# Placing identity, page pool and small vectors so that all matmul operands start at one residue of 512 bytes

## The chip, the cores and the metric

The kernel runs on one core of a Trainium2 chip. Five engines work side by side: TensorE (matmuls, transposes; the profile lists its weight loads apart, as PEld), VectorE (DVE), ScalarE (ACT), GpSimd (POOL) and SyncE (SP), which issues nearly all the DMAs here. Operands lie in the core's SBUF: 128 partitions, and in each a range of bytes; a tile has the same byte address in every partition. TensorE takes both operands from SBUF, the stationary one (loaded as weights, 128 columns) and the moving one (up to 512 columns), and writes to PSUM.

The metric is device microseconds of one execution, start to end. The kernel before takes 1100.9 us, the median of 3 runs (1098.44 to 1102.69 us).

## The reference

One encoder block over 1024 tokens of width 1024, in float32:

```python
n = rms_norm(h, norm1_g)
proj = n @ w_in                                   # 1024 x 2304: qa ka va qb kb vb
ya = mixer_a(qa, ka, va, sinks)                   # sliding window, ALiBi, sinks; 8 heads, 2 kv heads
yb = mixer_b(qb, kb, vb, rel_bias)                # own chunk + 8 before, relative bias; 8 heads
y = concatenate([rms_norm(ya, ga), rms_norm(yb, gb)])
h = h + y @ w_out                                 # 1024 x 1024
n2 = rms_norm(h, norm2_g)
u = square(relu(n2 @ w_ff1))                      # 1024 x 4096
h = h + u @ w_ff2                                 # 4096 x 1024
out = rms_norm(h, final_g)
```

## The kernel before

Every projection is a product of float32 accuracy made of three products of a shorter type: an operand is split into a high part (a copy of it, rounded) and a low part (what is left), and `mm3` (line 152) issues high x high, high x low and low x high, each a matmul with a stationary operand of 128 columns and a moving one of 512. `mm3` is called for the input projections (names `ip_...`), the output projection (`op_A`, `op_B`) and both MLP layers (`f`, and `f_a`, `f_b`, `f_c`). Scores (`S_...`) and the products of probabilities and V (`av_...`) are matmuls with 256 to 512 moving columns, and the probabilities are turned by transposes (`pt_...`; line 129), in which the data is the stationary operand and the identity the moving one, 128 columns.

The stages in time: input projections of the first heads (from 5 us on), attention with the other projections laid between its steps by a filler, output projection and second norm, the MLP's first layer (to about 778 us), its second layer with the final norm. Both MLP layers save an eighth of the products: seven products of half-size operands in place of eight, whose operands are sums of quarters. In the first layer (`product1`, line 907) the weights W are stationary and the transposed activations X are moving; in the second (`product2`, line 1072) the activations U are stationary and the weights V moving. A product of the second layer is 24 matmuls; the seven products are done for two slices of 512 each at a time, in the order of `order2` (line 1013). Operands are prepared two products ahead: VectorE makes the sums (T for the first layer, Z for the second, line 868), ScalarE copies the high parts (line 890), GpSimd or VectorE subtracts the low ones (line 132).

The order on every engine is set by the program's text, and on TensorE bound to it by `pe` (line 117). DMAs go through SP's one queue in order.

Tiles come from pools, and a pool's place in SBUF is set by the order in which pools are opened and by what each holds. In bytes per partition:

- `cp` (line 73), opened first: the identity (512 bytes), then the small vectors `ones`, `eps4`, `nsink`, `psink`, `ogc`, `g1c`, `warm` and `r1`, 32 bytes each.
- `main` (line 74): 35 pages of 4096 bytes (`page`, tag `pg`), 3 stage tiles (`stage`, tag `ws`) and 2 tiles of tag `tst`, 4096 bytes each. Pages hold the normed input nT, the projections' weights, Q, K, V, y, X, the high parts of W, u, w, C and more.
- `small` (line 75): statistics of one to eight columns, 32 bytes each at least, four buffers of a name; and a pad of 32 bytes (line 104).
- after `small`, one after another in the same place: `sp` (first loads), `at` (attention: the probabilities P, their turned parts T, bias, Y), `mp` (first layer: `page2`, tag `pg2`, with the low parts of W, and T and k), `fp` (second layer: `page3`, tag `pg3`).

In the second layer the first seven products have U and the high part of V in pages and the low part of V in a page or a stage tile; from the eighth on U (high and low) and the high part of V are of `page3`, the low part of V a stage tile (`high` and `third`, lines 1032 and 1033). Every slice that a matmul of the projections or the MLP takes out of a tile starts at a multiple of 512 bytes in it, so the residue of its address by 512 is that of its tile.

Of the kernel before, what the change touches and what calls it, by code (L numbers as in the profile page):

```python
# [8 lines left out]
F32 = mybir.dt.float32  # L9
# [6 lines left out]
P = 128  # L16
# [3 lines left out]
TB = SEQ // P  # L20
# [23 lines left out]
def kernel(  # L44
# [27 lines left out]

    cp = ctx.enter_context(tc.tile_pool(name="cp", bufs=1))
    main = ctx.enter_context(tc.tile_pool(name="main", bufs=1))
    small = ctx.enter_context(tc.tile_pool(name="small", bufs=4))
    dp = ctx.enter_context(tc.tile_pool(name="dp", bufs=1, space=DRAM))

# [3 lines left out]
    def page(shape, name, dt=F32R):  # L81
        return main.tile(shape, dt, tag="pg", bufs=NPAGES, name=name)
# [3 lines left out]

    ident = cp.tile([P, P], F32, name="ident")
    make_identity(nc, ident)
    ones = cp.tile([P, 1], F32, name="ones")
    nc.vector.memset(ones, 1.0)  # L90
    eps4 = cp.tile([P, 1], F32, name="eps4")
    nc.vector.memset(eps4, EPS / 4)
    nsink = cp.tile([P, 8], F32, name="nsink")
    psink = cp.tile([P, 8], F32, name="psink")
    ogc = cp.tile([P, 8], F32, name="ogc")
    g1c = cp.tile([P, 8], F32, name="g1c")
    nc.scalar.dma_start(g1c, norm1_g)
    warm = cp.tile([P, 1], F32, name="warm")
    nc.scalar.activation(warm, eps4, AF.Sqrt)

    last_load = [None]


    small.tile([P, 8], F32, tag="pad", bufs=1, name="pad")

    def load(dst, src, mark=False):

# [26 lines left out]
    def rstd(ss, n, width, name, r=None):  # L134

        if r is None:
            r = small.tile([P, width], F32, tag=f"rs{width}", name=f"r_{name}")
        u = small.tile([P, width], F32, tag=f"ru{width}", name=f"u_{name}")
        w = small.tile([P, width], F32, tag=f"rw{width}", name=f"w_{name}")
        q = small.tile([P, width], F32, tag=f"rq{width}", name=f"q_{name}")  # L140
        nc.scalar.activation(u, ss, AF.Sqrt, bias=eps4, scale=1.0 / (4 * n))
        nc.vector.tensor_scalar(w, ss, 1.0 / (4 * n), EPS / 4, ALU.mult, ALU.add)
        nc.vector.reciprocal(q, u)
        if width == 1:
            nc.vector.tensor_scalar(w, w, q, u, ALU.mult, ALU.add)
        else:
            nc.vector.tensor_tensor(w, w, q, ALU.mult)
            nc.vector.tensor_tensor(w, w, u, ALU.add)
        nc.vector.reciprocal(r, w)
        return r  # L150
# [37 lines left out]
    sp_ = ExitStack()  # L188
    sp = sp_.enter_context(tc.tile_pool(name="sp", bufs=1))
    sps = sp_.enter_context(tc.tile_pool(name="sps", bufs=1, space=PSUM))  # L190
    r1 = cp.tile([P, TB], F32, name="r1")
    R1 = page([P, SEQ], "R1", F32)
    xT_src = xT.rearrange("(k p) s -> p k s", p=P)
    nT = [[[page([P, 2, HALF], f"nT{t}{hl}{g}") for g in range(4)] for hl in range(2)] for t in range(2)]
# [13 lines left out]
    def token_scales(t):  # L208

        ss = small.tile([P, 4], F32, tag="ss4", name=f"ss1_{t}")  # L210
        for b in range(4):
            tb = 4 * t + b
            xr = sp.tile([P, D], F32, tag="xr", bufs=4, name=f"xr{tb}")
            load(xr, x[tb * P : (tb + 1) * P, :], True)
            nc.scalar.activation(xr, xr, AF.Square, accum_out=ss[:, b : b + 1])
        rstd(ss, D, 4, f"n1_{t}", r1[:, 4 * t : 4 * t + 4])
# [404 lines left out]
    def group_rstd(kind, psum, tag, bufs, r):  # L621
        ps = psum.tile([P, TB], F32, tag=tag, bufs=bufs, name=f"ss_{kind}")
        for tb in range(TB):
            matmul(ps[:, tb : tb + 1], sq[kind][:, tb * P : (tb + 1) * P], ones, start=True, stop=True)
        return rstd(ps, HALF, TB, f"g{kind}", r)
# [166 lines left out]
    def rows2(tb):  # L792

        h = hres.pop(tb)
        ps = flat(opb.pop(tb))
        nc.vector.scalar_tensor_tensor(ps, ps, rB[:, tb : tb + 1], h, ALU.mult, ALU.add)
        ss = small.tile([P, 1], F32, tag="ss", name=f"ss2_{tb}")
        nc.scalar.activation(h, ps, AF.Square, accum_out=ss)
        r = rstd(ss, D, 1, f"n2_{tb}")
        nc.scalar.activation(h, ps, AF.Copy)  # L800
        nc.sync.dma_start(hB[tb // 2][:, tb % 2], h)
        if tb in (4, 5):
            rows[tb] = main.tile([P, 2, HALF], F32, tag="tst", bufs=2, name=f"n2_{tb}")
        else:
            rows[tb] = page2([P, 2, HALF], f"n2_{tb}")
        nc.vector.scalar_tensor_tensor(flat(rows[tb]), ps, r, g2b, ALU.mult, ALU.mult)
# [394 lines left out]
def build(arrays):  # L1201
    import concourse.bacc as _bacc

    nc = _bacc.Bacc("TRN2", target_bir_lowering=False, num_devices=1)
    args = [nc.dram_tensor(f"in_{n}_dram", arrays[n].shape, F32, kind="ExternalInput").ap() for n in _INS]
    args.append(nc.dram_tensor("out_0_dram", (SEQ, D), F32, kind="ExternalOutput").ap())
    with tile.TileContext(nc, schedule_with_timeline_sim=True) as tc:
        kernel(tc, *args)
    return nc
# [9 lines left out]
```

## Time and profile before

| | before |
|---|---|
| median of 3 runs | 1100.9 us (1098.44 to 1102.69) |
| the profiled execution | 1100.78 us |
| its span, first to last instruction | 1099.0 us |
| TensorE busy | 1070.6 us, 97% |
| VectorE busy | 762.8 us, 69% |
| ScalarE busy | 530.4 us, 48% |
| GpSimd busy | 405.9 us, 37% |
| mean granted clock of TensorE | 0.997 of full |

A matmul's own duration in the profile is mostly latency, since matmuls are pipelined: one of 512 columns lasts 0.39 us and the next starts after 0.23 us. What a matmul costs in a row of them is therefore read from start to start: the start of a piece of the timeline less the start of the piece before, over the number of matmuls in it. In the chain of waits a piece's length is already counted so.

### The profile page before, as it was taken

The numbers are of one execution on the slowest core, as the hardware profiler recorded it, in microseconds if no ns is written. First come the engines' busy times: TensorE is split into PE (matmuls) and PEld (weight loads), VectorE is DVE, ScalarE is ACT, GpSimd is POOL, SyncE is SP. The second block draws the span as 40 slices with busy tenths as digits, with TensorE's granted clock in tenths as the row PEclk, the third lists the DMA queues.
The fourth block names the chain that finished last, engine by engine and source line by source line (L and its number), as shares of the span: only waits on it lengthen the run. The fifth ranks groups of instructions, "written<-read, shape, count | busy, mean of one in ns | idle before, by whom it ended". The sixth has DMA issues, their size and how long they took to land.

```text
span 1099.0 us, 14402 instructions
## 1 busy us (share of the span) xinstructions
PE 1070.6 (97%) x5088; PEld 879.8 (80%) x5088; DVE 762.8 (69%) x1170; ACT 530.4 (48%) x942; POOL 405.9 (37%) x248
## 2 busy tenths in 40 slices
PE   8998999999999999999999999999999999999997
PEld 6787878888878888778888888888787888888885
DVE  5577787767667766976755655646969777778667
ACT  7666765666564565553333333334333333333346
POOL 1365664343260231044553464445114024024025
PEclk9999999999999999999999999999999999999999
DMA  9943626353584342313354334516997535532004
GB/s 343 247 126 111 156 73 168 98 138 99 132 267 174 135 153 96 116 58 136 134 171 172 139 129 158 186 58 231 346 405 262 172 117 158 176 111 92 1 1 153
DMA packets 90584, 170.30 MB, mean 155 GB/s; under 512 B 7824, under 2 KB 43664, under 8 KB 90512
## 3 DMA queue, kind: packets, MB, share of 16 engines
q1 hardware_dynamic: 90368, 169.38, 46.7%
q8 instruction: 40, 0.66, 0.2%
q14 instruction: 32, 0.26, 0.1%
q10 hardware_dynamic: 144, 0.00, 0.0%
HBM read 105.39 MB, written 45.09 MB: 137 GB/s over the span
## 4 chain that ended last, share of the span: by engine, by line
PE 79%; DVE 10%; DMA 6%; issue 2%; ACT 2%; SPq 1%; DVEq 0%; ACTq 0%
PE f L126 25%; PE f_a L126 13%; PE f_c L126 6%; PE op_B L126 4%; PE ip_kB L126 4%; PE op_A L126 4%; PE f_b L126 3%; PE ip_qB L126 3%; PE ip_vB L126 3%; PE av_B L126 3%; PE ip_qA L126 2%; PE S_B L126 2%; PE pt_B L129 2%; DMA w<-in_w_ff_dram 2%; DVE Z L868 1%
## 5 line engine op out<-in xcount | busy, mean ns | idle before, releaser
L126 PE MATMUL f<-X,W 128*128 128x512 f32 x1344 | 316.1, 395 | 0.7 <-DVE k L936 0.7
L126 PEld LDWEIGHTS f<-X,W 128*128 128x128 f32 x1344 | 252.4, 189 | 56.1 <-issue 1.1
L126 PE MATMUL f_a<-V,U 128*128 128x512 f32 x768 | 180.5, 394 | 0.3 <-DVE V L132 0.3
L126 PEld LDWEIGHTS f_a<-V,U 128*128 128x128 f32 x768 | 144.1, 188 | 34.8 <-DVE V L132 0.7
L132 POOL TENSOR_TENSOR U<-u,U 128x1024 fp32r<-128x1024 f32 x32 | 81.0, 2531 | 234.9 <-PE f_c L126 140.9
L132 POOL TENSOR_TENSOR W<-T,W 128x1024 fp32r<-128x1024 f32 x32 | 82.9, 2591 | 163.2 <-ACT W L890 163.2
L126 PE MATMUL f_c<-V,U 128*128 128x512 f32 x384 | 90.3, 394 | 0.0
L126 PEld LDWEIGHTS f_c<-V,U 128*128 128x128 f32 x384 | 72.1, 188 | 16.9
L890 ACT ACTIVATE V<-Z 128x1024 fp32r<-128x1024 f32 x32 | 34.0, 1062 | 98.5 <-PE f_a L126 46.6
L132 POOL TENSOR_TENSOR W<-w,W 128x1024 fp32r<-128x1024 f32 x24 | 59.7, 2489 | 40.4 <-ACT W L890 37.6
L132 DVE TENSOR_TENSOR V<-w,V 128x1024 fp32r<-128x1024 f32 x24 | 47.9, 1998 | 28.4 <-ACT V L890 28.4
L890 ACT ACTIVATE V<-w 128x1024 fp32r<-128x1024 f32 x24 | 25.5, 1062 | 86.5 <-issue 36.3
L932 ACT ACTIVATE k<-f 128x1024 f32<-128x1024 f32 x24 | 24.7, 1028 | 81.6 <-PE f L126 81.6
L890 ACT ACTIVATE U<-u 128x1024 fp32r<-128x1024 f32 x56 | 58.5, 1044 | 8.7 <-DMA u<-ud 8.7
L388 ACT ACTIVATE P_B<-P_B,nm_B 128x640 f32<-128x640 f32 (+2 forms) x64 | 44.3, 693 | 25.6 <-DVE nm_B L387 13.2
L126 PE MATMUL ip_kB<-nT,w_kB 128*128 128x512 f32 x192 | 52.4, 402 | 3.1 <-DVE ts_qA L240 2.3
L890 ACT ACTIVATE W<-T 128x1024 fp32r<-128x1024 f32 x32 | 33.8, 1058 | 41.5 <-PE f L126 29.7
L126 PE MATMUL op_A<-w_o,y 128*128 128x512 f32 x192 | 52.1, 397 | 0.2 <-DVE h L705 0.2
L126 PE MATMUL ip_vB<-nT,w_vB 128*128 128x512 f32 x192 | 51.9, 398 | 0.0
L126 PE MATMUL ip_qB<-nT,w_qB 128*128 128x512 f32 x192 | 51.3, 395 | 0.0
L126 PE MATMUL ip_qA<-nT,w_qA 128*128 128x512 f32 x192 | 50.2, 399 | 0.9 <-DVE ts_qA L240 0.9
L132 DVE TENSOR_TENSOR V<-Z,V 128x1024 fp32r<-128x1024 f32 x32 | 46.2, 1447 | 6.8 <-ACT V L890 6.3
(208 smaller groups left out, 2018.9 us busy)
## 6 DMA issues: line engine op xcount, KB each, us to landing
w<-in_w_ff_dram SPq DMA_DIRECT2D x64, 512.0 KB, 4.5
u<-ud SPq DMA_DIRECT2D x56, 512.0 KB, 5.0
ud<-k SPq DMA_DIRECT2D x48, 512.0 KB, 2.7
KkB<-ts_kB SPq DMA_DIRECT2D x64, 128.0 KB, 2.3
yd<-y SPq DMA_DIRECT2D x14, 512.0 KB, 2.8
y<-yd SPq DMA_DIRECT2D x14, 512.0 KB, 7.1
xs<-in_xT_dram SPq DMA_DIRECT2D x16, 256.0 KB, 4.8
xr<-in_x_dram SPq DMA_DIRECT2D x8, 512.0 KB, 7.3
```

Of the source, the lines that this page charges most:

```text
L126: pe(nc.tensor.matmul(*args, **kw))
L129: pe(nc.tensor.transpose(*args))
L132: engine.tensor_tensor(lo, full, f(hi), ALU.subtract)
L388: nc.scalar.activation(pr[:, :n], pr[:, :n], AF.Exp, bias=nm, scale=-1.0, accum_out=sm)
L868: engine.tensor_tensor(t, a, b, op)
L890: nc.scalar.activation(w[0], full, AF.Copy)
L932: nc.scalar.activation(kept[p], ps, AF.Copy)
```

## The change

The identity stays in `cp` alone; the other small vectors go to a new pool `cv`, opened after `main`; the pad in `small` grows from 8 to 120 columns, and the scratch of `rstd` (u, w, q) gets two buffers in place of four. Nothing else is edited.

```diff
     cp = ctx.enter_context(tc.tile_pool(name="cp", bufs=1))
     main = ctx.enter_context(tc.tile_pool(name="main", bufs=1))
+    cv = ctx.enter_context(tc.tile_pool(name="cv", bufs=1))
     small = ctx.enter_context(tc.tile_pool(name="small", bufs=4))
...
     ident = cp.tile([P, P], F32, name="ident")
     make_identity(nc, ident)
-    ones = cp.tile([P, 1], F32, name="ones")
+    ones = cv.tile([P, 1], F32, name="ones")
...
-    g1c = cp.tile([P, 8], F32, name="g1c")
+    g1c = cv.tile([P, 8], F32, name="g1c")
...
-    small.tile([P, 8], F32, tag="pad", bufs=1, name="pad")
+    small.tile([P, 120], F32, tag="pad", bufs=1, name="pad")
...
-        u = small.tile([P, width], F32, tag=f"ru{width}", name=f"u_{name}")
-        w = small.tile([P, width], F32, tag=f"rw{width}", name=f"w_{name}")
-        q = small.tile([P, width], F32, tag=f"rq{width}", name=f"q_{name}")
+        u = small.tile([P, width], F32, tag=f"ru{width}", bufs=2, name=f"u_{name}")
+        w = small.tile([P, width], F32, tag=f"rw{width}", bufs=2, name=f"w_{name}")
+        q = small.tile([P, width], F32, tag=f"rq{width}", bufs=2, name=f"q_{name}")
...
-    r1 = cp.tile([P, TB], F32, name="r1")
+    r1 = cv.tile([P, TB], F32, name="r1")
```

The built program has the same instructions in the same order on every engine, with the same waits. What differs is the addresses (first byte of a partition, and that modulo 512):

| | before | after |
|---|---|---|
| identity | 16512, residue 128 | 16512, residue 128 |
| first page (35 pages, 4096 bytes each) | 17280, residue 384 | 17024, residue 128 |
| first stage tile (3, then 2 of `tst`) | 160640, residue 384 | 160384, residue 128 |
| start of `sp`, `at`, `mp`, `fp` | 184064, residue 256 | 183936, residue 128 |

The tiles in `sp`, `at`, `mp` and `fp` are 2048, 2560 or 4096 bytes, multiples of 512, so all of them share the residue of the pool's start.

## Rows read from the trace of the kernel before

**Rows 1.** The page: its span, and busy time of each engine.
```profile
span 1099.0 us, 14402 instructions
...
PE 1070.6 (97%) x5088; PEld 879.8 (80%) x5088; DVE 762.8 (69%) x1170; ACT 530.4 (48%) x942; POOL 405.9 (37%) x248
```

**Rows 2.** Chain of waits in the MLP: start us, length us, what, how many.
```profile
495.00 260.72 PE f L126 x1128
755.78 3.43 DVE T L868
...
798.54 10.15 DMA gfb<-in_final_norm_g_dram
808.76 11.46 DMA w<-in_w_ff_dram
...
844.94 22.43 PE f_a L126 x95
867.37 11.20 PE f_c L126 x48
...
1068.97 22.42 PE f_a L126 x96
```

**Rows 3.** Stretches: PE, PEld, DVE, ACT, POOL busy, clock, DMA share, GB/s.
```profile
495.00:755.80 260.80, 260.80 (x1131) 213.34 (x1130) 152.15 (x105) 91.36 (x91) 120.72 (x49) 1.00 0.43 152
755.80:845.00 89.20, 88.17 (x386) 71.94 (x384) 76.18 (x56) 32.58 (x33) 25.50 (x10) 1.00 0.84 310
845.00:1091.00 246.00, 246.00 (x1055) 197.99 (x1055) 182.56 (x165) 98.07 (x126) 68.82 (x32) 1.00 0.34 112
```

**Rows 4.** Waits of TensorE's MLP matmuls: total us, times, longest us.
```profile
PE f L126 <- DVE k L936: 0.7, 1, 0.7
...
PE f_a L126 <- DVE V L132: 0.3, 1, 0.3
```

**Rows 5.** TensorE's timeline, second layer's beginning: start us, us, matmuls.
```profile
778.70 11.04 PE L126 MATMUL f_a<-V,U 128*128 128x512 f32 x48
789.58 11.04 PE L126 MATMUL f_c<-V,U 128*128 128x512 f32 x48
...
822.28 11.15 PE L126 MATMUL f_a<-V,U 128*128 128x512 f32 x48
833.27 11.15 PE L126 MATMUL f_b<-V,U 128*128 128x512 f32 x48
...
844.94 5.39 PE L126 MATMUL f_a<-V,U 128*128 128x512 f32 x22 [0.30 <-DVE V L132]
```

**Rows 6.** Two stretches of the second layer, columns as in rows 3.
```profile
779.00:811.00 32.00, 32.00 (x143) 26.50 (x142) 28.18 (x23) 13.67 (x14) 6.86 (x2) 1.00 1.01 379
...
960.00:1065.00 105.00, 105.00 (x452) 84.51 (x451) 74.23 (x53) 37.71 (x38) 26.59 (x11) 1.00 0.17 56
```

**Rows 7.** Chain of waits, projections and transposes, to the first layer's start.
```profile
46.69 2.07 PE ip_qA L126 x9
...
122.75 1.37 PE ip_qB L126 x6
...
165.09 1.40 PE ip_kB L126 x6
...
438.65 0.44 PE tp L129 x4
...
444.57 10.93 PE op_B L126 x48
...
474.87 1.39 PE f L126 x6
```

**Rows 8.** TensorE's timeline, input projections.
```profile
30.22 5.60 PE L126 MATMUL ip_qA<-nT,w_qA 128*128 128x512 f32 x24
35.66 1.53 PE L126 MATMUL ip_vA<-nT,w_vA 128*128 128x512 f32 x6
```

**Rows 9.** The largest group of transposes: count, busy us, mean ns, idle before.
```profile
L129 PE MATMUL pt_B<-ident,P_B 128*128 128x128 f32 x240 | 42.2, 274 | 4.2 <-DMA y<-yd 2.4 <-DVE T_B L132 1.0 <-DVE rc_B L556 0.7
```

More of the change, by code (lines that the diff above doesn't have):

```diff
@@ L88 @@
     make_identity(nc, ident)
-    ones = cp.tile([P, 1], F32, name="ones")
+    ones = cv.tile([P, 1], F32, name="ones")
     nc.vector.memset(ones, 1.0)
-    eps4 = cp.tile([P, 1], F32, name="eps4")
+    eps4 = cv.tile([P, 1], F32, name="eps4")
     nc.vector.memset(eps4, EPS / 4)
-    nsink = cp.tile([P, 8], F32, name="nsink")
-    psink = cp.tile([P, 8], F32, name="psink")
-    ogc = cp.tile([P, 8], F32, name="ogc")
-    g1c = cp.tile([P, 8], F32, name="g1c")
+    nsink = cv.tile([P, 8], F32, name="nsink")
+    psink = cv.tile([P, 8], F32, name="psink")
+    ogc = cv.tile([P, 8], F32, name="ogc")
+    g1c = cv.tile([P, 8], F32, name="g1c")
     nc.scalar.dma_start(g1c, norm1_g)
-    warm = cp.tile([P, 1], F32, name="warm")
+    warm = cv.tile([P, 1], F32, name="warm")
     nc.scalar.activation(warm, eps4, AF.Sqrt)
+    small.tile([P, 120], F32, tag="pad", bufs=1, name="pad")
     last_load = [None]
-    small.tile([P, 8], F32, tag="pad", bufs=1, name="pad")
     def load(dst, src, mark=False):
```

## The prediction

> **What bounds the kernel now.** I read the busy shares first, to see which engine the span belongs to; then the chain of waits in order of time, to see where another engine holds TensorE up; then TensorE's timeline, for what one matmul costs in each stretch. The span is 1099.0 us of a profiled run of 1100.78 us, and TensorE is busy for 1070.6 us of it [rows 1]. From 495.00 to 755.78 us and from 844.94 us to the last matmul near 1091 us the chain is TensorE alone; between the two it runs over VectorE and DMA [rows 2]. VectorE has room in both TensorE stretches, 152.15 of 260.8 us and 182.56 of 246 us [rows 3]. The MLP's matmuls wait for an operand only twice, 0.7 and 0.3 us [rows 4]. So the time is the number of matmuls times what one costs, and this change touches neither the number nor the order: only the byte addresses of the operands.
>
> What the reader is to see is that a 128x512 matmul doesn't cost the same everywhere. In the second layer, 48 matmuls start at 778.70 us and the next 48 at 789.58 us: 10.88 / 48 = 226.7 ns each [rows 5]. From 822.28 to 833.27 us it is 10.99 / 48 = 229.0 ns [rows 5]. From 867.37 us to the end 48 take 11.20 us, 233.3 ns [rows 2]. In the first layer 1128 take 260.72 us, 231.1 ns [rows 2]. The granted clock is 1.00 in all these stretches (the 2.4 GHz level) [rows 3, 6], so the clock doesn't explain it. Nor does traffic: the fast stretch, 779 to 811 us, has the DMA engines full (1.01) and VectorE at 28.18 of 32 us, while 960 to 1065 us has DMA at 0.17 and is slow [rows 6].
>
> The placement does fit. Before the change a page lies at residue 384 of 512 bytes, a stage tile too, the attention and MLP pools at 256, the identity at 128. In the first layer X and the high weights are pages and the low weights lie at 256: 231.1 ns. In the second layer the first seven products have all operands in pages and stage tiles, and these are the matmuls of 226.7 ns; from the eighth on U and high V come from the pool at 256 and low V from a stage tile at 384: 229.0, later 233.3 ns. The output projection, whose weights and y are pages, takes 10.93 us for 48, 227.7 ns [rows 7]. The loads of the next weights overlap the running matmul (TensorE's two rows are 213.34 and 260.80 us in 260.8 us [rows 3]), so two reads of SBUF go on at once. I take it that where they start at different residues a matmul loses up to 6.7 ns more; that is a reading of three levels, and rival 1 is the other reading.
>
> **The change part by part.** The instruction lists, their order and their waits are those of before, engine by engine, so no operation is added, removed or moved. Three edits have one answer, nothing: the small vectors go to another pool, the pad grows, and the scratch of rstd gets two buffers in place of four (no wait appears in the built program, so no DVE or ACT row has cause to change). What is left is that identity, pages, stage tiles and the two big pools all come to residue 128.
>
> First layer: 1128 matmuls from 231.1 to 226.7 ns: 260.72 - 1128 x 0.22667 = 5.0 us. In the 22 us before it they stand in sixes behind transposes, such sixes at 1.39 us (the one at 474.87 us) against 6 x 226.7 = 1.36 [rows 7]; twelve of them, 0.3 us. This all lies on the chain.
>
> Second layer from 844.94 us: 95 + 864 + 96 = 1055 matmuls (the rows from 844.94, from 867.37 to 1068.97, and the last [rows 2]), at 233.3 to 226.7 ns: 1055 x 6.67 = 7.0 us. Cover for it: VectorE would be at 182.56 of 239 us.
>
> Between 755.78 and 844.94 us I count no gain. Its 386 matmuls would give up some 0.7 us (96 still of the first layer at 4.4 ns each, 168 of the second at none, 122 at 2.3), but the chain there is VectorE's T and Z, the load of gfb and the loads of w [rows 2], VectorE is busy 76.18 of 89.2 us and DMA 0.84 [rows 3], and TensorE arrives to find V missing at 844.94 us. It would only wait longer. The whole stretch is set off by a matmul at 755.78 us and so moves forward with the first layer; if its DMAs didn't, up to the 5 us would be lost there (second rival).
>
> Attention and projections, 0 to 473 us: about 1250 projection matmuls, in sixes of 1.37 to 1.40 us between transposes, scores and P V products [rows 7]. If all settled at 226.7 ns, some 208 sixes x 0.02 us = 4.2 us would go. That is the upper bound. Below: identity and P come to share a residue, which no transpose does now. Their interval is 0.44 us for four [rows 7]; there are 520 of them in seven groups, the largest of 240 [rows 9], and if each lost as much as a matmul does at most, 6.7 ns, that were 3.5 us. A break between matmuls that lie in pages alone, scores and projections at 46.69 us, also costs: nine take 2.07 us, not 2.04 [rows 7]. So most of the loss comes with the breaks, not with the residues, and I take 0.5 us, nearer to that row.
>
> Sum: 5.0 + 0.3 + 7.0 + 0 + 0.5 = 12.8 us, from 1100.8 us of the profiled run: 1088.0 us. The median of the three runs is 1100.9 us, so the two bases agree.
>
> A rule speaks against all of this. The row is that equal work costs 226.7 or 233.3 ns in one and the same layer [rows 2, 5]. The Trainium skill, "TensorE: Matmul & The Clock Gate", section "Step-by-step: what each phase is for", says that TensorE reads the streaming operand and the weights through two independent ports and that loading the next weights takes nothing from the running matmul. By that the addresses could not matter, the sum would be 0 and the time 1100.8 us; that is the first rival. The trace agrees in so far as loads and matmuls do overlap, and no page says what else would make the three levels.
>
> **The rivals.**
> 1. *Nothing changes: 1100.8 us, within 0.5%.* The levels would belong to the stages, not to the placement. For it: from 822 to 844 us the cost is 229.0 ns and from 845 us 233.3 ns with the same placement [rows 2, 5]; the change falls on the 0.30 us wait. So placement isn't all, there is a state that a break can shift. Against it: the change from 226.7 within a layer, at the same program text, falls on the product at which the buffers change. Chance 0.09.
> 2. *Only one layer gains.* If a stretch can stay in a worse state although its residues are equal, or the middle stretch eats the first layer's gain: only the second gives 1100.8 - 7.0 - 0.5 = 1093.3 us, only the first 1095.0 us. For it: the state above. Against it: the page-only rows come back to 226.7 and 227.7 ns after breaks (30.22 us: 24 matmuls to the next piece at 35.66 us, 5.44 / 24 = 226.7 [rows 8]; 10.93 / 48 [rows 7]). Chance 0.11.
> 3. *Slower: sharing is the bad case at 128.* What costs would be two reads that start at one place, with some luck at 384; with the identity there too and all at 128, every stream drops to the 233.3 level. First layer 1128 x 2.2 ns = 2.5 us, the second layer's 168 fast and 122 middling matmuls 1.1 + 0.5, attention 1250 x (233.3 - 230.0) = 4.1: together 8 us, 1109 us. It decides as soon as the mean over the MLP exceeds the present 231 to 232 ns. Against it: all page-only rows, whose operands share a residue, are the fastest there are. Chance 0.05.
> 4. *More than I count*: the sixes settle too and the transposes lose nothing, 1100.8 - 5.3 - 7.0 - 4.2 = 1084.3 us. Chance 0.04, in the forecast's direction.
>
> **How the numbers follow.** The forecast has 0.71. Its own range is 1084.3 (all of attention's excess) to 1092.0 us (transposes dearer by 3.5 and no 0.5). The range given reaches over rival 2 to 1095.0 us. A measurement of this kernel can tell about 0.5%, 5.5 us, from no change, so faster means below 1095.3 us: the forecast, rival 4 and nearly all of rival 2, 0.85. Within 0.5%: rival 1 and a rest, 0.10. Slower: 0.05.
>
> **What would show it.** In the changed profile the first layer's long piece should be 255.7 us for 1128 matmuls, not 260.72; each 48 of the second layer 10.88 us, not 11.20, from beginning to end, without a step where the buffers change; the wait for V before the thirteenth product longer than 0.30 us; the transposes at 0.44 us for four. If the first layer is still at 231 ns, placement isn't the cause there; if the middle stretch begins earlier but ends no earlier, its loads didn't move with TensorE; and if the 48s come to more than 11.20 us, the residue itself or its sharing is what costs.

## The result and the profile after

The changed kernel takes 1088.36 us (median of 4 runs, 1087.30 to 1090.49), the kernel before 1099.67 us over 4 runs (1098.29 to 1102.69): ratio 0.9896, 95% interval 0.9867 to 0.9925. The profiled execution took 1087.30 us, its span is 1085.5 us, 13.5 us under that of before.

The page of the changed kernel, busy us by engine (answers to [rows 1]):

```profile
span 1085.5 us, 14402 instructions
...
PE 1056.1 (97%) x5088; PEld 877.2 (81%) x5088; DVE 762.6 (70%) x1170; ACT 530.8 (49%) x942; POOL 408.1 (38%) x248
```

TensorE has the same 5088 matmuls and 14.5 us less to do; VectorE, ScalarE and GpSimd are where they were. So nothing was taken away: the same matmuls start closer together. The changed kernel's chain of waits in the MLP (start us, length us, what, how many; lines are one higher than before) answers to [rows 2]:

```profile
494.15 239.40 PE f L127 x1056
...
838.50 21.76 PE f_a L127 x96
860.26 10.88 PE f_c L127 x48
...
1056.13 21.79 PE f_a L127 x96
```

In the first layer 239.40 / 1056 = 226.7 ns (before: 231.1), in the late second layer 10.88 / 48 = 226.7 ns (before: 233.3). The timeline of TensorE at the second layer's beginning answers to [rows 5]:

```profile
767.53 5.69 PE L127 MATMUL f<-X,W 128*128 128x512 f32 x24 [1.34 <-DVE k L937]
773.05 11.04 PE L127 MATMUL f_a<-V,U 128*128 128x512 f32 x48
783.93 11.04 PE L127 MATMUL f_c<-V,U 128*128 128x512 f32 x48
...
827.46 11.04 PE L127 MATMUL f_b<-V,U 128*128 128x512 f32 x48
838.34 21.92 PE L127 MATMUL f_a<-V,U 128*128 128x512 f32 x96
```

From 773.05 us on the starts are 10.88 us apart (one 48, near 1023 us, takes 10.91). There is no step any more where the buffers change after the seventh product, and no wait for V at the thirteenth; the wait for k ahead of the second layer has grown from 0.74 to 1.34 us. The stretches, in columns as [rows 3]:

```profile
754.80:838.60 83.80, 82.46 (x365) 68.00 (x364) 74.88 (x55) 30.02 (x31) 23.93 (x9) 1.00 0.89 328
838.60:1077.50 238.90, 238.90 (x1055) 197.83 (x1054) 178.79 (x164) 98.44 (x126) 69.75 (x32) 1.00 0.34 112
```

The granted clock is 1.00 as before. VectorE is at 178.79 of 238.90 us in the late second layer, so it still leaves TensorE alone there. The 1055 matmuls that took 246 us take 238.9.

From the start times of both profiles, us: until the first layer's first matmul 450.4 and 449.7 (counted from TensorE's first); first layer 323.4 and 318.5, its waits included; second layer up to its thirteenth product 65.6 and 65.3; from there to the last matmul's start 246.7 and 239.2. The first and the third differ by little; the gain is 4.9 us in the first layer and 7.5 us in the late second, some 0.5 us of it the wait for V that is gone.

### The profile page after: what moved, and what is told of

Same layout as the page of the kernel before. It is cut to its first block, busy times and chain, and to the rows that moved or that the text cites. A ratio compares the mean times of both kernels' runs of the same rounds, so it can differ in the third digit from the quotient of the medians.

```text
span 1085.5 us, 14402 instructions
## 1 busy us (share of the span) xinstructions
PE 1056.1 (97%) x5088; PEld 877.2 (81%) x5088; DVE 762.6 (70%) x1170; ACT 530.8 (49%) x942; POOL 408.1 (38%) x248
## 4 chain that ended last, share of the span: by engine, by line
PE 87%; DVE 7%; DMA 2%; ACT 2%; issue 1%; POOL 1%; SPq 0%; DVEq 0%; ACTq 0%; POOLq 0%
PE f L127 24%; PE f_a L127 16%; PE f_c L127 8%; PE op_B L127 4%; PE f_b L127 4%; PE ip_kB L127 4%; PE op_A L127 4%; PE ip_qA L127 3%; PE ip_vB L127 3%; PE ip_qB L127 3%; PE av_B L127 3%; PE S_B L127 2%; PE pt_B L130 2%; PE S_A L127 1%; PE ip_kA L127 1%
## 5 line engine op out<-in xcount | busy, mean ns | idle before, releaser
L127 PE MATMUL f<-X,W 128*128 128x512 f32 x1344 | 310.5, 391 | 1.3 <-DVE k L937 1.3
L127 PE MATMUL f_a<-V,U 128*128 128x512 f32 x768 | 176.1, 389 | 0.0
```

Of the source, the lines that this page charges most:

```text
L127: pe(nc.tensor.matmul(*args, **kw))
```

## Experiments

Two readings stood against each other: a difference of address residues costs, whichever residue it is; or the residue 128, or the sharing with the identity, helps. Behind them stood rival 1, that the levels belong to a state and not to the placement. The first four runs take these apart.

**The pools alone put back to their old distance.** Edit to the changed kernel:

```diff
-    small.tile([P, 120], F32, tag="pad", bufs=1, name="pad")
+    small.tile([P, 88], F32, tag="pad", bufs=1, name="pad")
```

> The changed kernel with the pad at 88 columns: pages, stage tiles and identity stay at residue 128, and the pools of attention and MLP come 128 bytes lower, to residue 0, as far below the pages as before the change (256 against 384). If the difference between the two reads is what costs, the time is that of before, 1100 us, with 231.1 ns for a matmul of the first layer and 233.3 ns in the late second layer. If what helped was that pages lie at 128, or with the identity, it stays near 1088 us and 226.7 ns.

Measured: 1097.04 us, ratio to the kernel before 1.0005 (0.9983 to 1.0027; 10 runs against 20 of the kernel before taken along with them): the gain is gone. Its chain of waits:

```profile
493.08 244.08 PE f L127 x1056
842.72 21.97 PE f_a L127 x96
...
1029.50 11.07 PE f_c L127 x48
1040.57 11.09 PE f_a L127 x48
```

244.08 / 1056 = 231.1 ns, the first layer's old price to the digit. The second layer is not at the expected 233.3: 21.97 / 96 = 228.9 ns until 1029 us, then 11.09 / 48 = 231.0. So the pools' distance brings the loss back, but its size in the second layer isn't fixed.

**All at 384, the identity apart.** 256 bytes between identity and pages:

```diff
     make_identity(nc, ident)
+    cp.tile([P, 64], F32, name="shift")
```

> The changed kernel with 256 bytes laid between identity and pages: pages, stage tiles and all pools share residue 384, the identity alone stays at 128. If a shared residue is what counts, whichever it is and whatever the identity has, 1088 us and 226.7 ns in both MLP layers. If residue 128 itself or the identity's share in it matters, part of the 11 us comes back: 1092 to 1100 us.

Measured: 1088.82 us, ratio 0.9926 (0.9901 to 0.9950), 239.41 us for 1056 matmuls of the first layer, 226.7 ns in both layers. Residue 128 has no merit of its own, and the identity need not have the pages' residue by 512.

**The second layer's pool alone out of place.**

```diff
+    fp.tile([P, 32], F32, tag="off", bufs=1, name="off")
     gfb = fp.tile([P, D], F32, tag="gb", name="gfb")
```

> The changed kernel with 128 bytes put ahead of the second layer's pool alone: U and high V of the late second layer at residue 256, all else at 128. If each layer pays for its own placement, the first layer stays at 226.7 ns, the second returns to 229 and then 233.3 ns from its eighth product on, and the time is 1088 + 7 = 1095 us. If the late second layer was slow because of a state it fell into after the wait of 0.30 us, and no such wait comes, it stays at 226.7 to 229 ns and 1088 to 1091 us.

Measured: 1092.75 us, ratio 0.9962 (0.9944 to 0.9980), between the two times expected. Its chain of waits:

```profile
498.09 255.73 PE f L127 x1128
...
798.62 10.88 PE f_a L127 x48
...
820.45 10.99 PE f_a L127 x48
...
1040.27 11.09 PE f_a L127 x48
```

First layer 255.73 us for 1128 matmuls, 226.7 ns; second layer 226.7 ns for seven products, then 228.9 ns, from 1029 us on 231.1. Each layer pays for its own placement. But the other half of the expectation holds too: this trace has no wait for V, and the late second layer stays at 228.9 ns to 1029 us and never comes to 233.3. Placement decides that there is a loss; what came before has a say in how much.

**The disputed cost by itself.** A kernel of matmuls alone, weights set 0 to 480 bytes beside the moving operand:

> Not the block at all: 48 rows of 48 matmuls (128x512) alone on TensorE, with a copy of x as output in place of the result. Rows wa to wp: moving operand at residue 128, weights 0, 32, 64 ... 480 bytes above that residue. Rows va to vp: the same with the moving operand at 384. Rows ta to tp: the pattern of three of the first layer, only the third's weights shifted. If the difference of the residues sets the cost, wa and va are the cheapest at 226.7 ns, some others reach 231 to 240 ns, and w and v agree letter by letter. If the two reads never meet, all 48 rows cost the same. If it is a matter of the history, the rows differ without order, and w and v don't agree.

TensorE's timeline, the rows va to vj (start us, us, what, how many; a letter is 32 bytes of difference; the price of a row is the next start less its own, over 48):

```profile
186.35 11.05 PE L27 MATMUL va<-mov,sta 128*128 128x512 f32 x48
197.24 11.35 PE L27 MATMUL vb<-mov,sta 128*128 128x512 f32 x48
208.43 11.36 PE L27 MATMUL vc<-mov,sta 128*128 128x512 f32 x48
219.63 11.40 PE L27 MATMUL vd<-mov,sta 128*128 128x512 f32 x48
230.87 11.32 PE L27 MATMUL ve<-mov,sta 128*128 128x512 f32 x48
242.03 11.37 PE L27 MATMUL vf<-mov,sta 128*128 128x512 f32 x48
253.23 11.16 PE L27 MATMUL vg<-mov,sta 128*128 128x512 f32 x48
264.23 11.36 PE L27 MATMUL vh<-mov,sta 128*128 128x512 f32 x48
275.42 11.05 PE L27 MATMUL vi<-mov,sta 128*128 128x512 f32 x48
286.31 11.35 PE L27 MATMUL vj<-mov,sta 128*128 128x512 f32 x48
```

va: 10.89 / 48 = 226.9 ns; vb to vh 233.1, 233.3, 234.2, 232.5, 233.3, 229.2, 233.1; vi, at 256 bytes, 226.9 again, and vj is vb. The w rows agree letter by letter, but for the start of wa, the first row of all: its first matmuls start 427 ns apart, its last 24 are at 226.7. The t rows, the first layer's pattern, give 226.7 at 0 and at 256 bytes and at 128 bytes 11.10 / 48 = 231.2, the first layer's price in the block. Beside the v rows the other engines were idle and the DMA share was 0.00: the cost lies between TensorE's own two operands. And, in the 0 to 480 bytes tried, the period is 256 bytes, not the 512 of the prediction.

That asks two things of the whole kernel: whether 256 bytes apart is as good as 0, and whether the other half of the change was needed, since 128 and 384, the identity's and the pages' residues before the change, are equal by 256.

**Pools 256 bytes off.** The pad of the changed kernel at 56 columns.

> The changed kernel with the pad at 56 columns: pages, stage tiles and identity at residue 128, the pools of attention and MLP at 384, so 256 bytes apart by 512. The rows of matmuls alone gave 226.7 ns at 0 and at 256 bytes of difference and 228.9 to 234.4 ns at the fourteen others. If what counts is the residue by 256, this kernel runs as the changed one: 1088.5 us, 226.7 ns in both MLP layers, small spread. If the whole kernel needs the residue by 512, it is at 1094 to 1101 us.

Measured: 1090.54 us, ratio 0.9924 (0.9898 to 0.9950), 239.43 us for 1056 matmuls, 226.7 ns in both layers.

**The kernel before with the pad alone.**

```diff
-    small.tile([P, 8], F32, tag="pad", bufs=1, name="pad")
+    small.tile([P, 40], F32, tag="pad", bufs=1, name="pad")
```

> The kernel before with one edit, the pad from 8 to 40 columns: identity stays at 128, pages and stage tiles at 384, the pools move from 256 to 384; small vectors and scratch as before. By 256 everything then has residue 128. If the whole gain is the difference between pools and pages, 1088.5 us and 226.7 ns in both layers. If moving identity, pages or small vectors brought part of it, the time lies between this and 1097 us.

Measured: 1089.25 us, ratio 0.9922 (0.9893 to 0.9951); its chain:

```profile
495.52 239.41 PE f L126 x1056
839.81 21.76 PE f_a L126 x96
...
1057.43 21.77 PE f_a L126 x96
```

One number in the kernel before brings all of the gain in the MLP, and a time within the spread of the other kernels without a difference. Moving the small vectors and the pages wasn't needed.

**Which pair, and is there a memory.** A second kernel of matmuls alone:

> Not the block: rows of 48 (the last sixteen: 96) matmuls of 128x512 alone on TensorE, output a copy of x. ba to bh: both operands at the same residue, 128 to 352 in steps of 32 bytes: 226.7 ns in all if only the difference counts. oa to oh: two matmuls in turn, each matmul's own operands 0 to 224 bytes apart, but the weights loaded during it (the next one's) at its moving operand's residue. na to nh: own operands at the same residue, the weights loaded during it 0 to 224 bytes off. If what costs is the load of the next weights beside the running matmul, the o rows are all at 226.7 ns and the n rows from nb on at 229 to 236 ns; if it is something between a matmul and its own weights, the other way round. za to zp: all at one residue, each row begun by a matmul of 32, 64 ... 512 columns: 226.7 ns in all. ha to hp: the pattern of three of the late second layer with 128 bytes of difference, begun in the same way: if the level depends on what came before, the rows fall on more than one of 228.9, 231.1 and 233.3 ns.

Its timeline, some rows of each kind:

```profile
52.31 11.08 PE L27 MATMUL be<-mov,sta 128*128 128x512 f32 x48
63.22 11.08 PE L27 MATMUL bf<-mov,sta 128*128 128x512 f32 x48
...
129.02 11.20 PE L27 MATMUL od<-mov,sta 128*128 128x512 f32 x48
140.06 11.21 PE L27 MATMUL oe<-mov,sta 128*128 128x512 f32 x48
...
217.48 11.39 PE L27 MATMUL nd<-mov,sta 128*128 128x512 f32 x48
228.71 11.12 PE L27 MATMUL ne<-mov,sta 128*128 128x512 f32 x48
239.67 11.39 PE L27 MATMUL nf<-mov,sta 128*128 128x512 f32 x48
...
696.45 22.52 PE L27 MATMUL hl<-mov,sta 128*128 128x384 f32 x97
718.81 22.32 PE L27 MATMUL hm<-mov,sta 128*128 128x416 f32 x97
740.97 22.76 PE L27 MATMUL hn<-mov,sta 128*128 128x448 f32 x97
763.57 22.78 PE L27 MATMUL ho<-mov,sta 128*128 128x480 f32 x97
```

The b rows are all alike, 10.91 / 48 = 227.3 ns with the first few matmuls and 226.7 over their last 24: the common residue doesn't matter. The o rows from ob on settle at 230.0 to 231.7 ns (od: 11.04 / 48 = 230.0) and the n rows at 228.3 to 234.0 (nd: 11.23 / 48 = 234.0). I expected one kind to be free; neither is. So a matmul's own weights and the next one's both count, or the two can't be told apart by such rows, since with unequal weights the moving operand's start changes too; this stays open. The z rows, all at one residue, end at 226.7 ns whichever matmul began them. The h rows, the late second layer's pattern at 128 bytes, don't: over their last 24 matmuls, by their single starts, eight of them are at 231.1 ns (hl), seven at 233.3 (hn, ho), one at 228.8 (hm), and each keeps its level from its second dozen of matmuls to its end. What differs among them is the width of one matmul at the row's beginning, what was left by the row before, and which of two PSUM buffers the row writes.

**Both kernels once more.** If a level depends on how a row of matmuls begins, another execution of the kernel before may show other prices than the profile on which the sum was made.

> The kernel before, unchanged, profiled once more. The rows of matmuls alone fell on 228.9, 231.1 or 233.3 ns with 128 bytes of difference, depending on how they were begun, and on 226.7 ns only without difference. If the 233.3 ns of the late second layer in the first profile was one of such levels and not a fixed price, another execution may show 228.9 or 231.1 ns there, 2 to 5 us less. If it is a fixed price of that placement, 233.3 ns again.

> The same once more: the level of the late second layer is 228.9, 231.1 or 233.3 ns, the first layer's 231.1 or another of the three, never 226.7 ns; with a fixed price 231.1 and 233.3 ns as in the first profile.

> The changed kernel, profiled once more: 226.7 ns in both MLP layers in every execution, whatever it was begun with; what differs between executions lies in the waits ahead of the MLP and around its middle. With a level that can change as before, some stretch above 226.7 ns.

Measured in one execution each: 1097.53 and 1097.71 us for the kernel before, 1088.18 us for the changed one. Chains of the three, in that order:

```profile
494.32 244.08 PE f L126 x1056
844.59 22.22 PE f_a L126 x95
866.80 11.09 PE f_c L126 x48
...
1066.19 21.99 PE f_a L126 x96
```

```profile
496.36 244.08 PE f L126 x1056
846.11 21.97 PE f_a L126 x96
...
1032.88 11.07 PE f_c L126 x48
1043.96 11.09 PE f_a L126 x48
```

```profile
494.81 239.41 PE f L127 x1056
839.35 21.76 PE f_a L127 x96
...
1057.02 21.80 PE f_a L127 x96
```

The first layer of before is at 231.1 ns every time. Its late second layer was at 233.3 ns in the first profile; here it is at 231.1 and, from 1033 us on, at 228.9 (21.99 / 96 = 229.1), and in the third the other way round. From the thirteenth product to the last matmul's start that is 246.7, 243.9 and 242.0 us. The changed kernel needs 239.2 us both times. So its gain there is 7.5, 4.7 or 2.8 us, by the level that the kernel before is on.

What goes ahead of a change of level can be read from these traces. In all five with a difference in the late second layer (three of before, pools at 0, second layer's pool alone) the products from the eighth to the twelfth cost 228.9 ns. Two of them then wait for V at the thirteenth, the first profile of before for 0.30 us and the second for 0.28, in TensorE's timeline (start us, us, what, how many, the wait before it):

```profile
844.59 5.58 PE L126 MATMUL f_a<-V,U 128*128 128x512 f32 x23 [0.28 <-DVE V L132]
```

Behind the wait these two are at 233.3 and 231.1 ns; the three without it go on at 228.9. Later, between 1029 and 1039 us, within the 47th product, the level changes once more in all of them but the first, which stays at 233.3. In the changed kernel that product takes 228.0 and 229.5 ns a matmul in the two executions, and the next is back at 226.7. So the first change stands behind a wait, but nearly the same wait led to two levels, and no run sets such a wait on purpose; at the 47th product no wait is listed, and what shifts the level there stays open.

## Why the prediction was right, and where not

The forecast was 1088.0 us and the time is 1088.36; the mechanism named, a cost of different start addresses, is the one that the runs show. By its steps:

- *First layer, 5.0 us*: right, the start times give 323.4 and 318.5 us. Its sixes behind transposes, 0.3 us, gave nothing: they still take 1.39 us, like [rows 7].
- *Second layer, 7.0 us*: right for the pair of profiles (7.5 with the wait for V that went), but mis-sized as a price of the placement. I took the 233.3 ns of one execution as fixed, though [rows 5] showed 229.0 ns with the same placement and rival 1 named a state. The runs show three levels, so the term is 2.8 to 7.5 us. By the medians of the result the gain is 11.3 us; against the executions of before in the later runs (medians 1096.51 and 1097.39 us) it is 0.74 to 0.78% (ratios 0.9926, 0.9924 and 0.9922 of the three kernels without difference by 256), some 8 us, and not 12.8. That the time was hit all the same has a reason: base and term came from one execution, so its high level cancels in the time, though not in the gain. That the median of the first three runs, 1100.9 us, agreed with that execution was in part luck; of the kernel before only three executions were profiled, so the levels in the others aren't known.
- *Between 755.78 and 844.94 us, no gain*: nearly. Up to the thirteenth product it was 0.3 us. The wait for k grew by 0.60 us and ate that much of the first layer's gain; the prediction had put the longer wait at V. The wait for V, which I let grow, vanished here; in the kernels with all at 384 and with pools 256 bytes off it was 0.42 and 0.43 us, and the third profile of before has none either, so it comes and goes with the placement unchanged. The stretch as a whole moved forward with the first layer, its loads too, so the loss of rival 2 didn't come.
- *Attention, 0.5 us*: can't be read. The time ahead of the first layer is 449.7 us after and 450.4 before, but 448.4 to 453.6 us over all kernels here, by their waits. The projections' own cost didn't move: neighbours of `ip_vB` start 237.3 ns apart before and 237.7 after (149 pairs), those of `op_A` 235.1 and 235.5 (145). The bound below, dearer transposes, was needless: neighbours of `pt_B` start 111.3 and 110.9 ns apart (144 pairs).
- *The residue by 512*: the step that was wrong without harm. By 256 the identity and the pages agreed all along; only the pools of attention and MLP stood apart, and 32 more columns of pad bring the whole gain of the MLP.
- *The rivals*: rival 1 falls as a whole, the pad alone turns the levels on and off; its state is real, but only where residues differ. Rival 2's condition, a worse level at equal residues, didn't occur in the MLPs of the five profiles without difference by 256 (the changed kernel twice, all at 384, pools 256 bytes off, the pad alone), nor in the rows of matmuls at one residue. Rival 3 falls with the b rows. Rival 4 fell with the sixes.
- *The price of addresses at all*: the rows of matmuls alone cost 226.9 ns at equal residues and up to 234.2 at others, with nothing beside them but the weight loads. The Trainium skill, "TensorE: Matmul & The Clock Gate", section "Step-by-step: what each phase is for", has the two operands read through independent ports, by which the time would have stayed at 1100.8 us; as far as addresses go, these rows speak against it.

## What to carry to other kernels

Where TensorE is the bound, read a matmul's price from start to start in each stretch, and compare stretches that do the same work; equal work at two prices is worth a look at the addresses of both operands. Here it is enough that stationary and moving operands agree modulo 256 bytes, which a pad ahead of one pool brought about for 128 bytes of a partition; before moving anything else, try the pad alone. And before a price read from one execution goes into a sum, look for the same placement at another price in the same trace: if there is one, the term is a range.

## What the runs showed of the hardware

- A 128x512 matmul in float32r (the type of the split operands) with its own weight load starts every 226.7 ns at best, whatever the common residue (b rows, 128 to 352 bytes), and no difference of 0 to 480 bytes gave less. With a difference that isn't a multiple of 256 bytes it costs 228.3 to 234.2 ns over a row of 48.
- With a difference, in the patterns of three that `mm3` makes, the cost is a level out of several (228.9, 231.1, 233.3 ns at 128 bytes) that a run keeps over hundreds of matmuls. It changed behind a wait for V, with a row's beginning, and once in a program without a listed wait. From start to start a level is a sequence that repeats: about 226, 227 and 234 ns again and again at 228.9 (hm, third profile of before), 230, 236 and 234 at 233.3 (hk, first profile). Without a difference the cost came back to 226.7 ns after every beginning tried, within the first half of a row of 48 (z rows, whose last 24 are all at 226.7). That the 20 executions of the kernels without difference by 256 lie closer together (1087.3 to 1091.4 us) than the more than 40 with a difference in both layers (1093.6 to 1103.8 us) agrees with this, though these are more in number and the waits ahead of the MLP vary as well; with a difference in the late second layer alone it is 1089.0 to 1095.2 us.
- Why the period is 256 bytes, and which of a matmul's two neighbours in the weights it meets, was not settled.
